# A hybrid diffusion step on one core: two output rows in the input projection, nine begun strips, two-bank scores, Hyena beside five heads, and DeltaNet's last head three steps ahead

## The chip, the cores and the metric

The kernel runs on one core of a Trainium2 chip. The core has a matrix engine (TensorE, PE in the profile; its weight loads are PEld), a vector engine (DVE), a scalar engine (ACT), a general engine (POOL, also called GpSimd) and an engine that issues DMAs (SP). Engines run beside each other; each takes its own instructions in a fixed order and waits on semaphores for the others. SBUF is the on-chip memory, PSUM the accumulator memory of eight banks that the matrix engine writes. The metric is the device time of one execution in microseconds; lower is better.

## The reference

One inference step through two layers, on 128 context tokens and 512 latent tokens (640 rows together, model width 1024), in float32. Each layer is: half a SwiGLU feed-forward block (FFN, hidden width 2816), a mixer, another half FFN, each behind an RMSNorm with shift, scale and gate from a modulation vector.

```python
# layer 0's mixer: RWKV-7 (8 heads of 64) beside gated DeltaNet (4 heads of 128), both in both directions
p = p + mu * (centred_shift(p) - p)             # RWKV's input: a token and the mean of its neighbours
qkv = silu(conv3(qkv, conv_w))                  # DeltaNet's input: a three-tap convolution
S = S*w - (S kk)(kk a) + v k                    # RWKV's state, per token
S = S * exp(gl) + k_out @ (u - w @ S)           # DeltaNet's state, per chunk of 64 tokens
# layer 1's mixer: latent attention (8 heads) beside Hyena (order 2, width 512)
s = q_nope @ k_nope.T + q_pe @ k_pe.T
prob = softmax(s * scale); o = prob @ v
z = v
for gate in (x1, x2):                           # p -> conv3 -> v, x1, x2
    z = gate * (bidir_fftconv(z, h_f, h_b) + bias * z)
```

## The kernel before

Activations stand transposed: 128 partitions of features, 640 tokens along the free axis, cut into two halves of H = 320. A float32 product is made of three products of split operands: each operand x is a high part (rounded to a matmul-ready type by ACT) and a low part (x minus the high part, by DVE or POOL). A "strip" is 128 output columns of a projection: a load of 512 KB into a tile `wr` (two of them), the split into `wh` and `wl`, then 8 x 3 matmuls per half, 48 in all, into two PSUM banks.

*Order of the work.* The program is written in Python and unrolled. A planner (line `schedule_with_timeline_sim=True`) walks it ahead of time with a model of the engines' times and fixes each engine's order; program order is the priority, and work whose inputs are not ready in that model lets later work pass. Tiles come from pools with so many buffers per tag; an instruction that needs a buffer waits for the last use of the one that it replaces.

*FFN* (`ffn`, from L640 on). Gate and up projections are multiplied by a scheme of seven half-size products per 128 hidden columns instead of eight: `quarters` (L588) forms sums and differences of the activations' quarters, on POOL, DVE and ACT, when the second half's norm is ready; `strip` (L675) forms those of the weights on POOL (L684, tile `S`) and makes seven products of 12 matmuls each. Two of the seven products need only the first half's activations. `first` (L666) makes these two ahead for the first NE = 5 strips (here "begun strips"), so that TensorE has work while `quarters` runs; the results are kept in `u2` and `s1`. A begun strip loads its gate weights again later and then has five products left, 60 matmuls. The strips come in five groups (5, 4, 4, 4, 5), each followed by its part of the down projection. Beside the FFNs of layer 0 the modulation vectors of later blocks are computed from 256 KB pieces of their weights (`wmod`); `self.bg` is the list of those still to do.

*Layer 0's mixers* (`mixers0`). The input projection makes 15 RWKV strips (`shift`) and 17 of DeltaNet (`gate`, `conv`), each via a padded copy `pp` into an output row `o` (640 tokens) that is stored to DRAM (`pd`). In `shift` POOL adds the two neighbours (`nb`, L878), ACT scales the token itself (L881) and DVE adds both with one multiply-add per piece (L882); the pieces are the context and the latent tokens. `conv` uses `conv3`: ACT scales the token (L911), and two DVE multiply-adds per piece bring the neighbours (L912, L913). The tag `o` gets its number of buffers from the first call, in `shift`, which gives none, so there is one. Between the strips the heads' preparation runs, with the inversion of triangular blocks on DVE and POOL (L824, L826).

Then the recurrences run in steps of 64 tokens, forward and backward together (`chunks`). A head pair of RWKV and a head of DeltaNet form one set and take turns within a step, eight steps over the latent tokens and two over the context; `advance` lays consecutive sets one step over each other. After a set's last step, `tail` writes the RWKV tail (L1350 on) and the DeltaNet tail (L1600 on), whose rows go to `mixd`, from where the output projection (`out_proj`) loads them, DeltaNet's last head (row 7) before RWKV's last pair (row 3).

*Layer 1's mixers* (`mixers1`). `latents` makes the attention's compressed queries and keys and the values V. Then `heads` runs eight heads; for each it projects query and key, and for five blocks of 128 queries makes scores, softmax and values. Scores of a latent block are two products of 320 keys, each in a PSUM bank of its own (tag `sc`, four banks); DVE takes the maximum of each (L1746) and joins them (L1748), ACT makes two exponentials with row sums (L1752), DVE joins the sums (L1755) and scales (L1757). TensorE transposes the probabilities, and DVE copies them out of PSUM (`PT`, L1779). Beside heads 0 to 3 stand the twelve strips of Hyena's input (`hyena_in`, tiles `pp`, `cv`), three per head; then the weight pool is closed, Hyena's constants are loaded in its place, and the long convolutions (`hyena`) stand beside heads 4 to 7, three pieces of work per head out of seven, so that they are used up in head 6.

## Time and profile before

| what | value |
| --- | --- |
| time, median of 3 runs | 3182.38 us (3175.32 to 3186.39) |
| the profiled execution | 3187.08 us, its span 3185.1 us, granted clock 0.957 |
| busy share: TensorE, DVE, ACT, POOL | 93%, 71%, 43%, 38% |
| DMA | 385.36 MB, mean 121 GB/s |

The profile is one execution. Its page gives busy time by engine, the chain of work that ended last (followed back from the last instruction, at each step to what released it) and groups of equal instructions. The trace behind it answers for any stretch of time, tile or line: a table of stretches gives for each its length, then for TensorE, its weight loads, DVE, ACT and POOL the busy time and in brackets the number of instructions, then the granted TensorE clock (1.00 is full), the share of the DMA engines' time and the rate in GB/s. In a row such as `PE ps L287 <- DVE t L1735: 5.1, 1, 5.1` the instruction named first waited for the one behind the arrow, with total, count and longest in us. In timelines the first number is the start in us from the start of the span, the second the length; brackets hold the engine's idle time before it and what ended it. All matmuls are issued on line 287.

### The profile page before, as it was taken

How to read it: one execution, taken by the hardware profiler on the slowest of the kernel's cores; microseconds unless marked ns; L12 is line 12 of the kernel's file. 1: busy time of each engine (PE TensorE's matmuls, PEld its weight loads, DVE VectorE, ACT ScalarE, POOL GpSimd, SP SyncE). 2: the span in 40 equal slices, each digit the busy share in tenths (PEclk: the TensorE clock that was granted, in tenths of full speed). 3: DMA queues.
4: the chain of work that ended last, by engine and by line, in shares of the span. 5: the costliest groups of instructions: out<-in, count | busy, mean ns of one | idle time of the engine just before them, and what ended most of it. 6: DMA issues, size and time to landing. Idle time of an engine off the chain costs nothing.

```text
span 3185.1 us, 56006 instructions
## 1 busy us (share of the span) xinstructions
PE 2958.5 (93%) x21505; PEld 2671.5 (84%) x21505; DVE 2267.1 (71%) x4011; ACT 1355.0 (43%) x2846; POOL 1200.8 (38%) x1114
## 2 busy tenths in 40 slices
PE   7799999998988998889999979999989989899998
PEld 2689999987865676879999979999979748899998
DVE  5956667668769666695666797777766786977777
ACT  3423334566365555442333453333545424433333
POOL 1733335225545220263333474444310021744442
PEclk9999999998888989889999989999999989999999
DMA  7465542455564332445553222222321215222222
GB/s 273 137 209 164 177 137 72 166 157 170 139 151 112 93 86 81 161 146 181 163 180 116 82 93 87 84 86 83 122 62 58 91 47 181 67 90 86 80 83 83
DMA packets 277587, 385.36 MB, mean 121 GB/s; under 512 B 128704, under 2 KB 161120, under 8 KB 275400
## 3 DMA queue, kind: packets, MB, share of 16 engines
q1 hardware_dynamic: 277160, 381.13, 38.3%
q8 instruction: 169, 2.77, 0.4%
q14 instruction: 98, 0.80, 0.1%
q0 software_dynamic: 160, 0.66, 0.0%
HBM read 330.29 MB, written 51.42 MB: 120 GB/s over the span
## 4 chain that ended last, share of the span: by engine, by line
PE 54%; DVE 10%; ACT 4%; DMA 4%; POOL 3%; issue 3%; SPq 1%; DVEq 0%; ACTq 0%; POOLq 0%
PE ps L287 52%; DMA wr<-in_wd_dram 2%; DVE wl L655 1%; POOL S L684 1%; DMA wr<-in_wo_dram 1%; DVE nx L539 1%; DVE wl L471 1%; POOL X L826 0%; POOL wl L655 0%; POOL inv L824 0%; PE ps L1778 0%; DMA pd<-o 0%; DVE nacc L514 0%; DVE b L605 0%; ACT wh L470 0%
## 5 line engine op out<-in xcount | busy, mean ns | idle before, releaser
L287 PE MATMUL ps<-hh,wh 128*128 128x320 f32 x2208 | 698.6, 318 | 17.8 <-DVE g L1901 7.1
L287 PE MATMUL ps<-hl,wh 128*128 128x320 f32 x2208 | 695.1, 316 | 5.4 <-POOL hl L546 2.7
L287 PE MATMUL ps<-hh,wl 128*128 128x320 f32 x2208 | 686.5, 315 | 5.3 <-DVE wl L471 4.2
L287 PE MATMUL ps<-b,wh 128*128 128x320 f32 x2112 | 480.5, 315 | 32.5 <-DVE b L605 17.2
L287 PEld LDWEIGHTS ps<-hh,wh 128*128 128x128 f32 x2208 | 422.4, 192 | 34.4 <-DVE g L1901 7.9
L287 PEld LDWEIGHTS ps<-hl,wh 128*128 128x128 f32 x2208 | 422.8, 192 | 9.7 <-POOL hl L546 3.9
L287 PEld LDWEIGHTS ps<-hh,wl 128*128 128x128 f32 x2208 | 420.3, 191 | 8.8 <-DVE wl L471 5.4
L287 PEld LDWEIGHTS ps<-b,wh 128*128 128x128 f32 x2112 | 360.7, 192 | 40.5 <-DVE b L605 19.4
L287 PE MATMUL ps<-hidl,wh 128*128 128x320 f32 x1248 | 383.7, 309 | 0.0
L287 PE MATMUL ps<-hidh,wh 128*128 128x320 f32 x1248 | 383.2, 312 | 0.0
L287 PE MATMUL ps<-hidh,wl 128*128 128x320 f32 x1248 | 381.7, 309 | 1.0 <-DVE wl L471 1.0
L550 DVE SCALAR_TENSOR_TENSOR x<-ps,mod,x 128x128 f32<-128x128 f32 (+2 forms) x528 | 212.4, 435 | 212.3 <-PE ps L287 211.7
L655 POOL TENSOR_TENSOR wl<-S,wh 128x512 fp32r<-128x512 f32 x176 | 260.5, 1480 | 264.8 <-ACT wh L654 261.6
L684 POOL TENSOR_TENSOR S<-wr,wu 128x512 f32<-128x512 f32 x88 | 125.2, 1423 | 600.9 <-DMA wr<-in_wgu_dram 394.9
L287 PE MATMUL ps<-b,wl 128*128 128x320 f32 x1056 | 330.6, 315 | 9.4 <-DVE wl L655 6.1
L470 ACT CAST wh<-wr 128x512 fp32r<-128x512 f32 (+2 forms) x210 | 157.7, 754 | 407.0 <-PE ps L287 318.0
L654 ACT CAST wh<-S 128x512 fp32r<-128x512 f32 (+1 forms) x264 | 201.0, 763 | 216.0 <-PE ps L287 163.7
L471 DVE TENSOR_TENSOR wl<-wr,wh 128x512 fp32r<-128x512 f32 (+2 forms) x210 | 186.5, 891 | 82.9 <-ACT wh L470 80.9
L287 PEld LDWEIGHTS ps<-hidh,wh 128*128 128x128 f32 x1248 | 232.9, 188 | 13.3 <-issue 7.4
L287 PEld LDWEIGHTS ps<-hidh,wl 128*128 128x128 f32 x1248 | 233.4, 188 | 1.5 <-DVE wl L471 1.5
L287 PEld LDWEIGHTS ps<-hidl,wh 128*128 128x128 f32 x1248 | 234.1, 188 | 0.0
L287 PEld LDWEIGHTS ps<-b,wl 128*128 128x128 f32 x1056 | 202.3, 192 | 13.8 <-DVE wl L655 8.5
(457 smaller groups left out, 5971.2 us busy)
## 6 DMA issues: line engine op xcount, KB each, us to landing
wmod<-in_wmod_dram SPq DMA_DIRECT2D x288, 256.0 KB
wr<-in_wgu_dram SPq DMA_DIRECT2D x108, 512.0 KB
wu<-in_wgu_dram SPq DMA_DIRECT2D x88, 512.0 KB
wr<-in_wd_dram SPq DMA_DIRECT2D x80, 320.0 KB
wr<-in_wd_dram SPq DMA_DIRECT2D x96, 256.0 KB
pd<-o SPq DMA_DIRECT2D x32, 320.0 KB
wr<-in_abg_dram SPq DMA_DIRECT2D x17, 512.0 KB
wr<-in_wo_dram SPq DMA_DIRECT2D x16, 512.0 KB
```

Of the source, the lines that this page charges most:

```text
L287: self.nc.tensor.matmul(out=out, lhsT=lhsT, rhs=rhs, start=start, stop=stop)
L470: nc.scalar.copy(out=wh, in_=w)
L471: nc.vector.tensor_sub(out=wl, in0=w, in1=wh.bitcast(F32))
L539: nc.vector.scalar_tensor_tensor(out=xn[:, a:b], in0=self.x[c][:, k, a:b], scalar=A, in1=r[:, a:b], op0=ALU.mult, op1=ALU.mult)
L550: self.nc.vector.scalar_tensor_tensor(out=self.x[c][:, d, a:b], in0=q[:, a:b], scalar=gate[:, cond, d:d + 1], in1=self.x[c][:, d, a:b], op ...
L654: nc.scalar.copy(out=hi, in_=r)
L655: eng.tensor_tensor(out=lo, in0=r, in1=f32(hi), op=ALU.subtract)
L684: G.tensor_tensor(out=out, in0=x, in1=y, op=op)
```

## The change

Five edits, none of which changes what is computed.

1. *Out rows in two places.* The row `o` of the input projection gets two buffers, taken at the pool's opening, and `shift` uses `conv3` like `conv`: the tile `nb` and POOL's sum of the neighbours go, DVE has two multiply-adds per piece in place of one.
2. *Nine begun strips.* `NE` becomes (5, 9): an FFN begins nine strips if the list of modulation work is empty when it starts, else five. Strips 5 to 8 belong to the second group.
3. *Two-bank scores.* Both halves of a block's scores stand in one tile of two banks (two such tiles); one maximum and one exponential with one row sum run over both, and the joining instructions go. From head 3 on (`NHS`) ACT copies the transposed probabilities instead of DVE.
4. *Hyena beside five heads.* One of Hyena's input strips is placed in `latents` before the values, two behind them; three heads have three strips each; the convolutions stand beside heads 3 to 7 with two pieces each. The strips' pool opens earlier, on the other side of the memory.
5. *DeltaNet's lead.* In the last set (i == 3) DeltaNet's step s stands beside RWKV's step s - 3; a `yield True`, by which `advance` counts steps, comes only when RWKV has made one.

```diff
@@ constants
-NE = 5
+NE = (5, 9)
+NHS = 3
+LEAD = 3
@@ ffn
-        early = {}
+        early, ne = {}, NE[not self.bg]
...
-            p1, s1 = tile("u2", NE), tile("s1", NE + 1)
+            p1, s1 = tile("u2", ne), tile("s1", ne + 1)
...
-                for f in range(NE):
+                for f in range(ne):
                     first(f)
@@ in_proj0
+        out_ = lambda: self.t(ip, [P, T], "o", bufs=2)
+        for _ in range(2):
+            out_()
         pp = self.pads(ip, 2)
...
-            nb = self.t(ip, [P, T + 1], "nb")
-            nc.gpsimd.tensor_tensor(out=nb, in0=p[:, 0:T + 1], in1=p[:, 2:T + 3], op=ALU.add)
-            o = self.t(ip, [P, T], "o")
-            for a, b, g in ((0, LP, 0), (LP, T, 1)):
-                nc.scalar.activation(out=o[:, a:b], in_=p[:, a + 1 + g:b + 1 + g], func=AF.Copy, scale=omu[:, mi:mi + 1])
-                nc.vector.scalar_tensor_tensor(out=o[:, a:b], in0=nb[:, a + g:b + g], scalar=hmu[:, mi:mi + 1],
-                                               in1=o[:, a:b], op0=ALU.mult, op1=ALU.add)
+            o = out_()
+            self.conv3(p, (hmu[:, mi:mi + 1], omu[:, mi:mi + 1], hmu[:, mi:mi + 1]), o)
@@ chunks
-        for s in range(NCH - PCH):
-            sets = [[(W, 1, self.gdn_step(G, PCH + s, NCH - 1 - s, W[1], s < (NCH - PCH) // 2)),
-                     (S, 1, self.rwkv_step(R, y, PCH + s, NCH - 1 - s, S[1], s < (NCH - PCH) // 2))]]
+        n, lead = NCH - PCH, LEAD if i == 3 else 0
+        half = n // 2
+        for s in range(n + lead):
+            sets, r = [[], []], s - lead
+            if s < n:
+                sets[0].append((W, 1, self.gdn_step(G, PCH + s, NCH - 1 - s, W[1], s < half)))
+            if r >= 0:
+                sets[0].append((S, 1, self.rwkv_step(R, y, PCH + r, NCH - 1 - r, S[1], r < half)))
             if s < PCH:
-                sets.append([(W, 0, self.gdn_step(G, s, PCH - 1 - s, W[0], s < PCH // 2)),
-                             (S, 0, self.rwkv_step(R, y, s, PCH - 1 - s, S[0], s < PCH // 2))])
+                sets[1].append((W, 0, self.gdn_step(G, s, PCH - 1 - s, W[0], s < PCH // 2)))
+            if 0 <= r < PCH:
+                sets[1].append((S, 0, self.rwkv_step(R, y, r, PCH - 1 - r, S[0], r < PCH // 2)))
...
-            yield True
+            if r >= 0:
+                yield True
@@ latents
         latent(0, 3, "q_norm", put_q)
+        next(strips)
...
         self.close(ap)
+        for _ in range(2):
+            next(strips)
@@ softmax
-            ss = [self.ps("sc") for _ in keys]
...
+            sc = self.psum.tile([P, 2, 512], F32, tag="sc", name=self.name("ps"), bufs=2)[:, :len(keys)]
+            n = keys[0][1]
...
+            for i, (k0, _) in enumerate(keys):
+                self.mm(sc[:, i, :n], qt[hh][:96, P * qi:P * qi + P], kt[hh][:96, k0:k0 + n])
+            nc.vector.tensor_reduce(out=mx, in_=sc[:, :, :n], axis=mybir.AxisListType.XY, op=ALU.max)
...
+            nc.scalar.activation(out=pr[:, :nk].rearrange("p (k n) -> p k n", n=n), in_=sc[:, :, :n], func=AF.Exp, scale=scale, bias=mx,
+                                 accum_out=sm)
@@ values
-                nc.vector.tensor_copy(out=PT[hh][:, g:g + n, P * (qi - 1):P * qi],
-                                      in_=q[:, :P * n].rearrange("p (k t) -> p k t", k=n))
+                (nc.vector.tensor_copy if hh < NHS else nc.scalar.copy)(out=PT[hh][:, g:g + n, P * (qi - 1):P * qi],
+                                                                        in_=q[:, :P * n].rearrange("p (k t) -> p k t", k=n))
@@ mixers1
-        self.latents(h, first)
+        sp = self.pool("strips", bufs=1, reuse_waits="tile")
+        strips = self.hyena_in(h, sp)
+        self.latents(h, first, strips)
...
-        for i in range(4):
+        for i in range(NHS):
             next(heads)
             for _ in range(3):
                 next(strips)
...
-        for i in range(4, 8):
+        for i in range(NHS, 8):
             next(heads)
-            for _ in range(3):
+            for _ in range(2):
                 next(conv, None)
```

More of the change, by code (lines that the diff above doesn't have):

```diff
@@ L690, in strip @@
             else:
-                u, g0 = tile("u2", NE), tile("s1", NE + 1)
+                u, g0 = tile("u2", ne), tile("s1", ne + 1)
                 a11, a12 = parts((g, V))
@@ L852, in gate @@
             q = self.strip(I["abg"][0], h)
-            o = self.t(ip, [P, T], "o", bufs=2)
+            o = out_()
             for c in range(2):
@@ L860, in conv @@
             q = self.strip(I["abg"][1 + i], h)
-            o = self.t(ip, [P, T], "o", bufs=2)
+            o = out_()
             if j == 3:
@@ L876, in shift @@
             self.padded(q, p)
[L877 to L883 removed]
+            o = out_()
+            self.conv3(p, (hmu[:, mi:mi + 1], omu[:, mi:mi + 1], hmu[:, mi:mi + 1]), o)
             if func is not None:
@@ L1244, in chunks @@
                         to, j, steps = run
-                        r = next(steps, False)
-                        if r is False:
+                        got = next(steps, False)
+                        if got is False:
                             runs.remove(run)
-                        elif r is not None:
-                            to[j] = r
+                        elif got is not None:
+                            to[j] = got
                     yield
+            if r == PCH - 1:
+                nc.sync.dma_start(out=self.O["s_rwkv"][:, i].rearrange("d p v -> p d v"), in_=S[0])
             if s == PCH - 1:
-                nc.sync.dma_start(out=self.O["s_rwkv"][:, i].rearrange("d p v -> p d v"), in_=S[0])
                 for d in range(2):
                     nc.sync.dma_start(out=self.O["s_gdn"][d, i], in_=W[0][d])
-            yield True
+            if r >= 0:
+                yield True
     def rwkv_step(self, X, ys, c0, c1, S, first):
@@ L1633, in small_split, with latents @@
         return out
-    def latents(self, h, first):
+    def latents(self, h, first, strips):
         nc, I = self.nc, self.I
@@ L1740, in softmax @@
             nk = sum(n for _, n in keys)
[L1741 to L1757 removed]
+            sc = self.psum.tile([P, 2, 512], F32, tag="sc", name=self.name("ps"), bufs=2)[:, :len(keys)]
+            n = keys[0][1]
+            mx = self.t(ap, [P, 1], "mxs", bufs=4)
+            sm = self.t(ap, [P, 1], "sms", bufs=4)
+            for i, (k0, _) in enumerate(keys):
+                self.mm(sc[:, i, :n], qt[hh][:96, P * qi:P * qi + P], kt[hh][:96, k0:k0 + n])
+            nc.vector.tensor_reduce(out=mx, in_=sc[:, :, :n], axis=mybir.AxisListType.XY, op=ALU.max)
+            nc.vector.tensor_scalar(out=mx, in0=mx, scalar1=-scale, scalar2=None, op0=ALU.mult)
+            pr = S[hh, qi] = self.t(ap, [P, 2 * H], "pr", bufs=2)
+            nc.scalar.activation(out=pr[:, :nk].rearrange("p (k n) -> p k n", n=n), in_=sc[:, :, :n], func=AF.Exp, scale=scale, bias=mx,
+                                 accum_out=sm)
+            nc.vector.reciprocal(out=sm, in_=sm)
+            nc.vector.tensor_scalar(out=pr[:, :nk], in0=pr[:, :nk], scalar1=sm, scalar2=None, op0=ALU.mult)
         def values(hh, qi):
@@ L1923, in hyena_in @@
                 for g, n in ((0, 4), (4, 1)):
-                    q = self.ps("tr")
+                    q = self.ps("tr" if "tr" in self.tags else "mx")
                     for j in range(n):
@@ L2116, in mixers1 @@
         self.l1 = self.pool("l1", bufs=1, reuse_waits="tile")
-        self.latents(h, first)
+        self.tc.swap_default_side()
+        sp = self.pool("strips", bufs=1, reuse_waits="tile")
+        self.tc.swap_default_side()
+        strips = self.hyena_in(h, sp)
+        self.latents(h, first, strips)
         self.banks(mm=2, sc=4, tr=2)
         ap = self.pool("heads", bufs=1, reuse_waits="tile")
-        sp = self.pool("strips", bufs=1, reuse_waits="tile")
-        heads, strips = self.heads(ap), self.hyena_in(h, sp)
-        for i in range(4):
+        heads = self.heads(ap)
+        for i in range(NHS):
             self.mark(f"head{i}")
@@ L2128, in mixers1 @@
         next(strips, None)
+        self.tc.swap_default_side()
         self.close(sp)
+        self.tc.swap_default_side()
         self.close_w()
```

15 lines of the change are left out of this document (removed).

## The prediction, made before the result was known

> **What bounds the kernel now.** I read the totals of the page first, then a table of time stretches cut at the places that the change touches (columns: length, then busy time and instruction count of the TensorE matmuls, the weight loads, DVE, ACT and POOL, then granted clock, DMA share, GB/s), then the waits, groups and timelines inside those stretches.
>
> ```profile
> PE 2958.5 (93%) x21505; PEld 2671.5 (84%) x21505; DVE 2267.1 (71%) x4011; ACT 1355.0 (43%) x2846; POOL 1200.8 (38%) x1114
> ...
> 590.00:900.00 310.00, 273.23 (x2033) 259.99 (x2033) 200.38 (x338) 168.31 (x337) 132.79 (x221) 0.92 0.52 150
> ...
> 1200.00:1252.00 52.00, 49.97 (x612) 38.32 (x612) 34.82 (x114) 32.41 (x118) 2.13 (x4) 1.00 0.24 72
> 1252.00:1300.00 48.00, 33.04 (x142) 25.36 (x142) 24.56 (x60) 18.37 (x43) 5.14 (x7) 0.65 0.47 156
> 1836.00:1890.00 54.00, 35.02 (x191) 31.64 (x190) 50.65 (x45) 30.98 (x55) 42.36 (x24) 0.81 0.30 102
> ...
> 1960.00:2006.00 46.00, 46.00 (x316) 46.00 (x315) 33.75 (x47) 19.02 (x32) 28.48 (x20) 1.00 0.24 74
> 2730.00:2760.00 30.00, 21.14 (x107) 19.47 (x106) 29.08 (x24) 16.40 (x26) 24.84 (x11) 0.83 0.19 65
> 2760.00:2800.00 40.00, 35.74 (x228) 33.11 (x227) 39.45 (x45) 13.40 (x23) 31.89 (x21) 1.00 0.28 95
> 2320.00:2372.00 52.00, 45.37 (x264) 41.48 (x263) 31.66 (x32) 20.16 (x30) 8.42 (x6) 0.97 0.24 71
> 2372.00:2517.00 145.00, 144.53 (x925) 133.37 (x926) 98.34 (x247) 72.28 (x198) 11.96 (x9) 0.99 0.15 46
> 2517.00:2658.00 141.00, 122.31 (x469) 71.18 (x468) 115.76 (x261) 33.54 (x103) 28.53 (x20) 0.94 0.26 89
> ```
>
> TensorE bounds the kernel: it is busy 93% of the span, and in the middle of an FFN (1960 to 2006) it never stops: 316 matmuls in 46 us, **0.1456 us per 128x320 matmul**. Nothing in the change lowers the number of matmuls. So each edit can win only what TensorE now loses in its stretch: 36.8 us in the input projection (310 less 273.23), 15.0 at the end of layer 0's mixers (48 less 33.04, at a clock of 0.65), 19.0 and 8.9 where the last two FFNs begin, and 6.6 + 0.5 + 18.7 = 25.8 in the attention and Hyena stage. In the two FFN beginnings DVE is full (50.65 of 54, 29.08 of 30); in the Hyena stretch it has 115.76 of 141.
>
> **Scores, strips and Hyena (2320 to 2658).** The rows are groups of DVE and ACT instructions in the Hyena stretch (count, busy, mean ns), then TensorE's waits in the three stretches.
>
> ```profile
> L1746 DVE TENSOR_REDUCE mxs<-ps 128x1 f32<-128x320 f32 (+1 forms) x35 | 15.6, 466 | 0.1
> L1779 DVE COPY PT<-ps 128x512 f32<-128x512 f32 (+1 forms) x32 | 14.4, 484 | 0.6 <-PE ps L1778 0.6
> ...
> L1755 DVE TENSOR_TENSOR sms<-sms 128x1 f32<-128x1 f32 x16 | 6.2, 388 | 1.8 <-ACT pr L1752 1.5
> ...
> L1748 DVE TENSOR_TENSOR mxs<-mxs 128x1 f32<-128x1 f32 x16 | 3.3, 206 | 0.0
> ```
> ```profile
> L1752 ACT ACTIVATE pr<-ps,mxs 128x320 f32<-128x320 f32 (+1 forms) x35 | 17.7, 510 | 46.0 <-PE ps L1778 25.3 <-DVE mxs L1749 20.7
> L1752 ACT ACTIVATION_READ_ACCUMULATOR pr<-ps,mxs 128x1 f32 x35 | 6.9, 197 | 0.0
> ...
> L1787 ACT COPY om<-ps 128x512 f32<-128x512 f32 x3 | 1.8, 586 | 22.1 <-PE ps L287 22.1
> ```
> ```profile
> PE ps L287 <- POOL acc L1660: 3.7, 1, 3.7
> ...
> PE ps L287 <- DVE t L1735: 5.1, 1, 5.1
> ...
> PE ps L287 <- DVE t L1735: 5.6, 1, 5.6
> ```
>
> Now twelve Hyena strips stand beside heads 0 to 3, where TensorE is full anyway (144.53 of 145), while heads 4 to 7 share 141 us with the whole of Hyena, where DVE lags and TensorE twice waits over 5 us for the query's rotary product queued behind Hyena's products. The change moves three strips ahead into the latents, which wait 3.7 us for a POOL sum, and gives Hyena five heads. A strip is 48 matmuls, 48 x 0.1456 = 7.0 us; a head without strips is at most (145 - 12 x 7.0) / 4 = 15.3 us of TensorE. The latents get 21 us more to do, the strip heads 36 less, the Hyena stretch 15.3 more: zero in sum, so the gain is idle time that closes.
>
> Does DVE permit it? In the Hyena stretch four heads now carry 14.4 us of copies of transposed probabilities, 6.2 and 3.3 of joining halves. From head 3 on all three leave DVE: 23.9 off. The added head brings a quarter of what stays in its groups; the reductions are 15.6 / 4 = 3.9, and I allow 10 with its other small groups. 115.8 - 23.9 + 10 = 102 us in about 141 + 15 - 15 = 141: 72%, against 82%. The merged operations are in no row. A reduction over both banks costs between one half (0.47) and two (0.93), the joint exponential between 0.51 and 2 x (0.51 + 0.20) = 1.41; I take the upper ends, so no gain for them, and the lower would free another 20 x 0.47 = 9 us of DVE. ACT takes 20 large and 20 small copies, at most 40 x 0.586 = 23 us on 33.54: it stays below half. If ACT's cover failed, those 23 us would be on the path. The moved strips issue their 512 KB loads and, for the last four, stores on SP's queue, at DMA shares of 0.24 and 0.15.
>
> TensorE keeps some idle: the last head still stands alone, and Hyena's chain still has its turns. Of 25.8 I leave 8 open: **-18**, bounds -26 (all closed) and +37 (the slower rival below).
>
> **Out rows (590 to 900).** Waits (us in total, times, longest), the two operations that change places (ns least/median/most), and pieces of the chain (start, length).
>
> ```profile
> ACT o L911 <- DMA pd<-o: 35.1, 9, 11.9
> ...
> ACT o L881 <- DMA pd<-o: 22.4, 9, 6.0
> ...
> PE ps L287 <- ACT w L1051: 10.0, 2, 9.1
> ```
> ```profile
> L913 DVE SCALAR_TENSOR_TENSOR o<-pp,cols,o x24: 247/634/911, 636.1 to 893.7; 128x128 f32<-128x128 f32 x12, 128x512 f32<-128x512 f32 x12
> ```
> ```profile
> L878 POOL TENSOR_TENSOR nb<-pp x15: 1254/1924/2235, 604.9 to 868.7; 128x641 f32<-128x641 f32 x15
> ```
> ```profile
> 739.80 5.13 DMA pd<-o
> ...
> 836.02 4.53 DMA pd<-o
> ...
> 895.96 2.42 DMA pd<-o
> ```
>
> One row `o` holds a finished strip until its store has landed; ACT, in order, waits over 57 us for it, and behind ACT once TensorE (9.1 us). On the chain these stores stand for 5.13 + 4.53 + 2.42 = 12.1 us. With a second row, a store has a whole strip more, 7.0 us, to land in 5.1. That removes at most 12.1. The sum of neighbours leaves POOL (15 x 1.924 = 28.9 us, POOL also solving the block inverses there) and becomes one more multiply-add per piece on DVE: 30 x 0.634 = 19.0 us. DVE has 200 of 310 us, so it lies beside TensorE; uncovered it would be +19.0 - 12.1 = +7. I take **-7**, bounds -12 and +7. The weight loads issue on SP behind the same stores as before; nothing new queues there.
>
> **The last head's lead (1200 to 1300).** DVE instructions (start, length): the RWKV state's last write, DeltaNet's state writes, the ends of both tails.
>
> ```profile
> 1250.33 0.46 DVE L1326 SCALAR_TENSOR_TENSOR S<-ps,eG,Se 128x64 f32<-128x64 f32 x2
> ...
> 1263.26 0.35 DVE L1584 SCALAR_TENSOR_TENSOR W<-W,eGl,ps 128x128 f32<-128x128 f32 x1 [0.75 <-PE ps L287]
> ...
> 1267.92 0.49 DVE L1371 TENSOR_TENSOR ys<-ys,ps 128x320 f32<-128x320 f32 x1 [1.27 <-PE ps L287]
> ...
> 1271.10 0.35 DVE L1584 SCALAR_TENSOR_TENSOR W<-W,eGl,ps 128x128 f32<-128x128 f32 x1 [0.25 <-PE ps L287]
> ...
> 1278.33 0.48 DVE L1623 SCALAR_TENSOR_TENSOR tt<-ps,cols,tt 128x64 f32<-128x64 f32 x2 [0.63 <-PE ps L1618]
> ```
>
> The last row is the end of DeltaNet's tail, at 1278.8; RWKV's tail ended at 1268.4, 17.6 us after its state at 1250.8. DeltaNet's state came 20.6 us later. Three steps of lead turn this round: DeltaNet's tail runs under RWKV's last steps, and RWKV's tail ends the stage. If RWKV isn't delayed, the stage ends 10.4 us earlier; if both end in the middle, RWKV 10.3 later, nothing is gained. If DeltaNet's three steps simply go first at their latency, 3 x 7.8 (1263.26 to 1271.10), RWKV ends at 1250.8 + 23.5 and the stage at 1291.9: +13. TensorE was full at 1200 to 1252, so some delay is sure: **-4**, bounds -10 and +13. The states' stores move with their own recurrence on SP's queue; they are late for nobody.
>
> **Nine begun strips (1836 and 2730).**
>
> ```profile
> L655 DVE TENSOR_TENSOR wl<-S,wh x88: 1206/1210/2290, 123.9 to 3122.8; 128x1024 fp32r<-128x1024 f32 x88
> ```
> ```profile
> 2742.62 0.48 DVE L673 TENSOR_TENSOR s<-ps,u 128x320 f32<-128x320 f32 x1
> 2743.02 1.48 DVE L605 TENSOR_TENSOR b<-hidh,b 128x1280 fp32r<-128x1280 f32 x1
> ...
> 2749.76 4.87 DVE L605 TENSOR_TENSOR b<-hidh,b 128x1280 fp32r<-128x1280 f32 x2 [0.92 <-ACT b L604]
> ```
> ```profile
> L415 SPq DMA_DIRECT2D wmod<-in_wmod_dram x288: 327/382/1672, 7.1 to 1715.7; - x144
> ```
>
> The two subtractions of one shape show why DVE is full here: alone the 128x1280 form takes 1.48 us, beside POOL 4.87 / 2 = 2.43. The Trainium skill, page "SBUF — State Buffer", section "Who interferes with whom", says that a DVE instruction with two SBUF inputs and a GpSimd one that reads SBUF exclude each other; by that rule the trace agrees, and it speaks against bringing more such splits into this place. It would give the upper of the prices that follow; the row's own spread gives them without it.
>
> The modulation weights are all loaded by 1715.7, so the list is empty at 1836 and 2730 and both of layer 1's FFNs begin nine strips; layer 0's keep five. Four more bring 96 matmuls (14.0 us) forward, plus four loads of 512 KB that are read twice. On DVE each brings a split of weights (1.21 to 2.29) and an addition (0.48) forward: 6.8 to 11.1 us, on an engine that has 3.4 us free in the first beginning and 0.9 in the second. So the beginning ends 3 to 10 us later. Later the four strips have 60 matmuls instead of 84; a begun strip takes 40 x 60 / 228 = 10.5 us (DVE-bound), a whole one 46 x 84 / 316 = 12.2, so 6.8 us come back, not 14. That is 6.8 - 3.4 - 6.8 = -3.4 and -0.9 with the low price: **-4** together; bounds -28 (2 x 14.0, if both engines had room) and +8 (2 x 11.1 - 2 x 6.8). Queued behind the four loads on SP is strip 0's, which POOL needs first.
>
> **Sum.** -18 - 7 - 4 - 4 = -33 on the profiled execution's 3187.08 us (span 3185.1 and 2.0 around it): 3154.1. The runs' median, 3182.38, lies 4.7 below the profiled execution; so 3149.4 for the median, 3149.
>
> **Rivals.**
> 1. *The idle moves on* (16 in 100). In the Hyena stretch a head's own chain takes over: ACT's copies and the joint exponential in one queue, TensorE waiting for probabilities. For it: ACT there waits 25.3 us for transposes and 20.7 for maxima. Against: no TensorE wait on exponentials in the listed waits. The -18 falls to -3, with DVE's extra work in the input projection eating half its -7: 3182.4 - 3 - 3.5 - 4 - 4 = 3168 at best, and with the begun strips at +8 3180: no change or barely faster.
> 2. *The scores' banks* (9 in 100, slower). Two one-bank tiles per block now fall free one by one; the pair falls free only after one joint exponential, and the maximum starts only after the second product. If TensorE has nothing else queued before the next scores, each of 32 wide blocks costs 0.51 + 0.20 + 0.47 = 1.18 us: +37.7. It decides from the point where TensorE waits for ACT in front of scores. Against: 925 matmuls at 144.53 of 145 with the present chain. 3149.4 + 18 + 37.7 = 3205.
> 3. *The begun strips lock with POOL* (5 in 100 as the deciding part). Each of DVE's added splits takes its longest length while POOL reads beside it: +8 by the bound, and if strip 0's loads come four turns later another 4 x 2.29 in each FFN, +26 in all instead of -4: 3149.4 + 30 = 3179, no change. The Trainium skill ("SBUF — State Buffer", "Who interferes with whom") has this exclusion as a rule.
> 4. *The lead does not lead*: order is planned ahead, and the steps could be put back where they were. 0 instead of -4, 3153; inside the forecast.
>
> **Chances.** Forecast with its own range 3120 to 3170: 70 in 100; rival 1: 16, rival 2: 9, rival 3: 5. About 0.3%, 9.5 us, is what a measurement can tell from no change. Faster (below 3172.8): 0.70 and half of rival 1, 0.78; slower (above 3191.9): 0.08; the same: 0.14. The range goes from 3120 (a further 29: idle all closed in the attention stage -8, stores -5, lead -6, strips -10) to 3182, the upper end of rival 1.
>
> **What would show it.** Right: no ACT waits on `pd<-o` above 2 us each; TensorE idle under 10 us from the latents to the end of attention; DeltaNet's tail done before RWKV's; matmuls in the two FFN beginnings where TensorE stood. Wrong: TensorE waiting for exponentials, begun strips spaced over 11 us in the second group, DVE in front of TensorE in the input projection, or RWKV's last state after 1270.

## The result and the profile after

The changed kernel takes 3154.74 us (median of 4 runs, 3151.82 to 3158.72) against 3183.58 for the kernel before beside it (3175.32 to 3186.39): a ratio of **0.9914**, 95% interval 0.9892 to 0.9936. The ratio makes it some 27 us less, the two medians 28.8. The profiled execution took 3158.72 us, its span 3157.0 at a granted clock of 0.962. The forecast of 3149 lies 6 us below; the sum was nearly right. Its terms were not: two of the four were worth nothing that can be measured, and one of the two priced lowest brought about half of the gain. That the sum came out is luck.

Totals of the page after. DVE did 35.5 us less than before and POOL 25; TensorE has the same 21505 matmuls and is busy 13.6 us less, at a mean clock of 0.962 against 0.957.

```profile
PE 2944.9 (93%) x21505; PEld 2662.6 (84%) x21505; DVE 2231.6 (71%) x3905; ACT 1363.8 (43%) x2823; POOL 1175.8 (37%) x1099
```

To see where the time went I cut both executions at DVE instructions that stand in both: the last reciprocal of the norm ahead of layer 0's mixers, the last written out row, the last tail, the norm ahead of layer 1's first FFN, the norm ahead of the latents, the first split for the output projection, and the final norm (start, length, instruction). The first fence is the timeline of the kernel before; its out row (893.7) and last tail (1278.33) are quoted in the prediction. The second is the changed kernel.

```profile
591.09 2.15 DVE L514 RECIPROCAL nacc<-nacc 128x320 f32<-128x320 f32 x1 [4.15 <-ACT nacc L513]
...
1851.32 2.15 DVE L514 RECIPROCAL nacc<-nacc 128x320 f32<-128x320 f32 x1 [0.29 <-ACT nacc L513]
...
2286.97 2.15 DVE L514 RECIPROCAL nacc<-nacc 128x320 f32<-128x320 f32 x1 [0.89 <-ACT nacc L513]
...
2662.18 1.69 DVE L476 TENSOR_TENSOR hl<-m,hh 128x320 fp32r<-128x320 f32 x4
...
3162.28 2.15 DVE L514 RECIPROCAL nacc<-nacc 128x320 f32<-128x320 f32 x1 [0.89 <-ACT nacc L513]
```
```profile
592.50 2.15 DVE L516 RECIPROCAL nacc<-nacc 128x320 f32<-128x320 f32 x1 [4.15 <-ACT nacc L515]
...
879.40 0.75 DVE L914 SCALAR_TENSOR_TENSOR o<-pp,cols,o 128x512 f32<-128x512 f32 x1
...
1272.76 0.48 DVE L1633 SCALAR_TENSOR_TENSOR tt<-ps,cols,tt 128x64 f32<-128x64 f32 x2 [0.63 <-PE ps L1628]
...
1849.26 2.15 DVE L516 RECIPROCAL nacc<-nacc 128x320 f32<-128x320 f32 x1 [0.29 <-ACT nacc L515]
...
2279.24 2.15 DVE L516 RECIPROCAL nacc<-nacc 128x320 f32<-128x320 f32 x1 [0.88 <-ACT nacc L515]
...
2641.51 1.69 DVE L478 TENSOR_TENSOR hl<-m,hh 128x320 fp32r<-128x320 f32 x4
...
3134.14 2.15 DVE L516 RECIPROCAL nacc<-nacc 128x320 f32<-128x320 f32 x1 [0.89 <-ACT nacc L515]
```

The differences of these rows are the stages in the table. The other rows are the same cuts through the profiles of the experiments that follow; the last column is each run's ratio to the kernel before, timed beside it, with its interval. "Rows" is the part of the front up to the last out row.

| kernel | rows | front, to the last tail | first FFN of layer 1 | attention and Hyena | output projection and second FFN, to the final norm | ratio |
| --- | --- | --- | --- | --- | --- | --- |
| before | 302.6 | 687.7 | 435.6 | 375.2 | 500.1 | 1 |
| changed | 286.9 | 680.7 | 430.0 | 362.3 | 492.6 | 0.9914 (0.9892 to 0.9936) |
| five begun strips (ne5) | 285.6 | 680.2 | 433.6 | 365.8 | 500.4 | 0.9968 (0.9956 to 0.9980) |
| nine places, five begun (buf9) | 286.2 | 675.4 | 434.3 | 366.9 | 500.5 | 0.9956 (0.9939 to 0.9972) |
| eleven begun, no lead (ne11_no_lead) | 286.3 | 677.4 | 427.2 | 362.2 | 488.0 | 0.9880 (0.9861 to 0.9899) |
| no lead | 288.6 | 680.7 | 431.0 | 364.3 | 491.6 | 0.9912 (0.9896 to 0.9927) |
| old rows | 303.2 | 677.9 | 429.8 | 367.3 | 491.6 | 0.9941 (0.9923 to 0.9958) |
| one place | 303.3 | 692.2 | 432.1 | 361.0 | 491.9 | 0.9936 (0.9919 to 0.9953) |
| old rows, no lead (old_front) | 302.8 | 673.4 | 430.4 | 365.0 | 492.8 | 0.9919 (0.9903 to 0.9936) |
| old attention and Hyena (old_mla) | 285.9 | 674.5 | 430.1 | 378.0 | 493.3 | 0.9963 (0.9950 to 0.9975) |
| old scores | 286.5 | 675.5 | 427.4 | 375.8 | 491.5 | 0.9943 (0.9927 to 0.9959) |
| copies on DVE (pt_dve) | 286.4 | 679.0 | 428.8 | 371.9 | 491.1 | 0.9929 (0.9912 to 0.9945) |
| Hyena beside four heads (hyena4) | 286.7 | 671.8 | 428.9 | 363.3 | 492.2 | 0.9922 (0.9908 to 0.9936) |
| no maxima (no_max) | 286.4 | 683.2 | 428.4 | 359.7 | 491.6 | 0.9901 (0.9884 to 0.9919) |

The table is the main instrument of this study: a stage that keeps its instructions shows how far it moves by itself. The second FFN with nine begun strips takes 491.1 to 493.3 us in ten profiles, with five 500.1 to 500.5 in three: 8.3 us, far outside the scatter; the first FFN takes 427.4 to 432.1 with nine, 433.6 to 435.6 with five. ("Second FFN" in what follows includes the output projection ahead of it.) The front, with instructions in the same order in eight profiles (changed, ne5, buf9, old_mla, old_scores, pt_dve, hyena4, no_max), takes 671.8 to 683.2: there a difference of 7 us between two profiles proves nothing.

The front's column stops at the last tail, and that flatters the new rows. In the changed kernel the first weights of the output projection that follows land only after the tails, as ACT's wait for them shows; with the old rows (before, old_rows, old_front) the same instruction stands 3.2 us ahead of the last tail's end and waits for nothing.

```profile
1273.91 1.04 ACT L472 CAST kh<-wr 128x1024 fp32r<-128x1024 f32 x1 [1.26 <-DMA wr<-in_wo_dram]
```

From the norm to the first split for that projection it is 687.6 us before, 683.8 changed, and 673.3 with the whole front as before (old_front).

The two stretches in which TensorE stood before, as tables of stretches: first the FFN beginning of layer 1's first FFN, before and after; then the attention stage after, begun and divided at the same events as in the prediction's table, and the input projection (length, busy time and count of TensorE, its weight loads, DVE, ACT, POOL, then clock, DMA share, GB/s).

```profile
1850.00:1870.00 20.00, 18.97 (x115) 18.25 (x114) 17.78 (x20) 12.04 (x21) 10.96 (x5) 0.91 0.32 105
1870.00:1890.00 20.00, 10.67 (x51) 9.21 (x50) 18.97 (x10) 9.67 (x12) 19.92 (x9) 0.74 0.15 52
```
```profile
1850.00:1870.00 20.00, 17.45 (x110) 16.66 (x109) 19.33 (x20) 15.07 (x24) 5.63 (x2) 0.96 0.23 79
1870.00:1890.00 20.00, 16.89 (x99) 16.12 (x100) 12.70 (x14) 9.88 (x17) 8.34 (x5) 0.91 0.50 158
...
2312.20:2385.00 72.80, 70.16 (x446) 66.74 (x445) 42.53 (x52) 33.50 (x59) 8.74 (x6) 1.00 0.24 75
2385.00:2490.00 105.00, 104.86 (x674) 95.62 (x673) 65.64 (x147) 47.85 (x117) 8.72 (x7) 1.00 0.14 44
2490.00:2642.00 152.00, 132.11 (x542) 80.71 (x540) 110.57 (x211) 54.00 (x135) 32.90 (x22) 0.97 0.27 92
...
590.00:900.00 310.00, 273.63 (x2064) 258.31 (x2063) 215.55 (x376) 174.40 (x356) 121.40 (x230) 0.93 0.53 155
```

The latents are now full (70.16 of 72.8, where 45.37 of 52 stood), and the FFN beginning holds 209 matmuls in 40 us in place of 166. In the Hyena stretch TensorE still stands 19.9 of 152 us; DVE has 110.57 there, 73%, close to the predicted 72%, and yet TensorE waits. The prediction's table stops 4.2 us ahead of the first split for the output projection; with the same end for both, half a microsecond behind that split, the whole stage before and after is:

```profile
2320.00:2662.70 342.70, 313.11 (x1658) 246.53 (x1657) 248.56 (x544) 129.06 (x334) 48.91 (x35) 0.96 0.22 70
2312.20:2642.00 329.80, 307.13 (x1658) 243.07 (x1656) 218.74 (x408) 135.35 (x310) 50.37 (x35) 0.99 0.22 73
```

The same 1658 matmuls: of 12.9 us, 6.9 were idle time of TensorE (29.6 to 22.7) and 6.0 busy time, at a clock of 0.99 in place of 0.96.

### The profile page after: what moved, and what is told of

It reads as the page before. It is cut to its first block, busy times and chain, and to the rows that moved or that the text cites. A ratio compares the mean times of both kernels' runs of the same rounds, so it can differ in the third digit from the quotient of the medians.

```text
span 3157.0 us, 55877 instructions
## 1 busy us (share of the span) xinstructions
PE 2944.9 (93%) x21505; PEld 2662.6 (84%) x21505; DVE 2231.6 (71%) x3905; ACT 1363.8 (43%) x2823; POOL 1175.8 (37%) x1099
## 4 chain that ended last, share of the span: by engine, by line
PE 47%; DVE 9%; DMA 3%; issue 2%; ACT 2%; POOL 1%; SPq 0%; DVEq 0%; ACTq 0%; POOLq 0%
PE ps L289 46%; DMA wr<-in_wd_dram 2%; DVE wl L657 1%; DMA wr<-in_wo_dram 1%; DVE nx L541 1%; DVE wl L473 0%; DVE hidl L478 0%; DVE nacc L516 0%; PE ps L1788 0%; DVE nacc L508 0%; DVE u L689 0%; DVE nx L712 0%; ACT wh L656 0%; DVE b L607 0%; DVE nsq L689 0%
## 5 line engine op out<-in xcount | busy, mean ns | idle before, releaser
L289 PE MATMUL ps<-hh,wh 128*128 128x320 f32 x2208 | 693.4, 316 | 14.3 <-DVE g L1912 7.1
L289 PEld LDWEIGHTS ps<-hh,wl 128*128 128x128 f32 x2208 | 418.4, 191 | 13.1 <-DVE wl L657 6.0
L289 PEld LDWEIGHTS ps<-hl,wh 128*128 128x128 f32 x2208 | 420.6, 191 | 10.1 <-DVE hl L607 3.9
```

The lines of the kernel that those rows point to most:

```text
L289: self.nc.tensor.matmul(out=out, lhsT=lhsT, rhs=rhs, start=start, stop=stop)
```

## The experiments

**1. Begun strips.** Three kernels: five begun strips again; nine places for their parts but five begun; eleven begun (without the lead of the last head, for which experiment 2 shows no gain; it has eleven places as well).

```diff
-NE = (5, 9)
+NE = (5, 5)      # ne5
+NE = (5, 11)     # ne11_no_lead, with LEAD = 0
@@ buf9
-                for f in range(ne):
+                for f in range(5):
```

> The changed kernel with five begun strips in both FFNs of layer 1 again; all else stays changed. Theory (the two traces): nine begun strips won 4.9 us in the first of these FFNs and 8.3 in the second, so without them the time is 3154.7 + 13 = 3168, ratio to the kernel before about 0.9955. Rival (the price of the prediction, DVE-bound): they won 4 in all: 3159, ratio 0.993.

> The changed kernel with nine places for the parts of begun strips in layer 1, but only five strips begun. Theory (work carried ahead): the gain is the 96 matmuls brought forward, the places alone bring nothing, so the ratio to the kernel before is that of the run with five begun strips, 0.997. Rival (the places): strips that are further apart no longer wait for a place to come free, and the ratio is that of the changed kernel, 0.9914.

> The changed kernel with eleven begun strips in layer 1's FFNs and without the lead of the last head. Theory (work carried ahead pays as long as TensorE stands still in the beginning): four strips won 13 to 17 us in two FFNs, 1.6 to 2.1 each per FFN; about 8.5 and 7 us of idle are left there beside the wait for the first product, so two more strips win half to all of that rate, 3 to 8 us: ratio 0.9912 less 0.001 to 0.0025, about 0.9895. Rival (DVE, full in the beginning, is the bound and two more splits of 1.2 us each are simply added): the ratio stays at 0.9912 or rises to 0.992.

With five the ratio is 0.9968, and both FFNs fall back to their old length. The theory holds and the prediction's price does not: by the stages nine strips are worth 434.5 - 429.7 = 4.8 us (means of three and ten profiles) and 8.3 us. Places alone bring nothing: 434.3, 500.5 and 0.9956, as with five. Eleven bring a further 2.5 and 4.0 us and the fastest kernel of the study, 0.9880, median 3143.07 against 3178.63 beside it. Per strip that is (2.5 + 4.0) / 2 = 3.3 us over both FFNs, against 13.1 / 4 = 3.3 from five to nine: no sign of a price that rises. But eleven is one profile, and its 427.2 in the first FFN lies only 0.2 below the shortest with nine; the second FFN, 3.1 below, and the ratio carry the reading.

Where it comes back is read from the ends of the strips. The timelines give the first of the two multiplications that close a strip (L708), for strips 4, 5, 8 and 9 of the second FFN: first with five begun strips, then with nine.

```profile
2788.72 0.48 DVE L708 TENSOR_TENSOR nsq<-nsq,s 128x320 f32<-128x320 f32 x1
2833.60 1.57 DVE L708 TENSOR_TENSOR nsq<-nsq,s 128x320 f32<-128x320 f32 x1
...
2869.34 0.48 DVE L708 TENSOR_TENSOR nsq<-nsq,s 128x320 f32<-128x320 f32 x1
2911.03 1.58 DVE L708 TENSOR_TENSOR nsq<-nsq,s 128x320 f32<-128x320 f32 x1
```
```profile
2791.07 0.48 DVE L708 TENSOR_TENSOR nsq<-nsq,s 128x320 f32<-128x320 f32 x1
2831.91 1.07 DVE L708 TENSOR_TENSOR nsq<-nsq,s 128x320 f32<-128x320 f32 x1
...
2862.82 0.48 DVE L708 TENSOR_TENSOR nsq<-nsq,s 128x320 f32<-128x320 f32 x1
2901.33 1.58 DVE L708 TENSOR_TENSOR nsq<-nsq,s 128x320 f32<-128x320 f32 x1
```

Counted from the output projection's first split (2643.14 and 2641.51), strip 4 gets there at 145.6 with five and 149.6 with nine: the beginning is **4.0 us later**. Then across the down projection to strip 5: 44.9 against 40.8, 4.0 back. Strips 5 to 8: 35.7 against 30.9, 4.8 back. To strip 9, across the next down projection: 41.7 against 38.5, 3.2 back. In sum 12.0 of the 14.0 us of matmuls that were carried forward come back. In the first FFN the same four steps are 9.4 later, and 3.8, 6.1 and 3.1 back. That TensorE had room in the beginning shows in its counts up to strip 4: 921 matmuls in 149.6 us, 142.8 busy at a clock of 0.96, in place of 831 in 145.6, 130.7 busy at 0.92.

One reason why the beginning got only 4 to 9 us later is seen in the splits themselves: the row of the nine weight splits in the first FFN's beginning (least, median, most in ns), then timeline rows of DVE and of POOL there.

```profile
L657 DVE TENSOR_TENSOR wl<-wr,wh x9: 1209/1214/3820, 1834.7 to 1878.8; 128x1024 fp32r<-128x1024 f32 x9
```
```profile
1866.42 3.82 DVE L657 TENSOR_TENSOR wl<-wr,wh 128x1024 fp32r<-128x1024 f32 x1
```
```profile
1866.24 2.91 POOL L620 TENSOR_TENSOR hidl<-hidl,hidh 128x1280 f32<-128x1280 f32 x1 [13.52 <-DVE hidh L618]
```

More than half of the splits took 1.21 us, eight of the nine at most 1.9. The one of 3.82 started 0.2 us into a POOL sum of 2.91. (The second FFN has one like it: 3.55 us, begun 1.4 us into a sum of 3.83.) POOL was busy only 5.63 and 8.34 us in the two stretches of 20: it stood waiting for DVE's quarters (13.52 us) while the begun strips were split. The Trainium skill ("SBUF — State Buffer", "Who interferes with whom") has the exclusion of a DVE instruction with two SBUF inputs and a GpSimd one that reads SBUF as a rule; the trace agrees in these two rows, and shows that there was little POOL work to exclude.

**2. The lead.**

```diff
-LEAD = 3
+LEAD = 0
```

> The changed kernel with DeltaNet's and RWKV's steps of the last head side by side again. Theory: on the two chains the loads of the output weights set the start of the output projection, and the stage moved by 1 us only beyond what it had inherited: 3154.7 + 1 = 3156, ratio 0.992. Rival (the prediction): the lead is worth 4: 3159, ratio 0.993. If the weights' loads are what waits, the last tails end later by some 5 us in this run's trace and the output projection still starts within 2 us of where it does in the changed kernel.

0.9912: no difference. Timeline rows of the last state writes and tails, first of the changed kernel, then without the lead:

```profile
1250.82 0.48 DVE L1336 SCALAR_TENSOR_TENSOR S<-ps,eG,Se 128x64 f32<-128x64 f32 x2
...
1260.22 0.35 DVE L1594 SCALAR_TENSOR_TENSOR W<-W,eGl,ps 128x128 f32<-128x128 f32 x1
...
1269.56 0.49 DVE L1381 TENSOR_TENSOR ys<-ys,ps 128x320 f32<-128x320 f32 x1
```
```profile
1264.28 0.35 DVE L1594 SCALAR_TENSOR_TENSOR W<-W,eGl,ps 128x128 f32<-128x128 f32 x1 [0.76 <-PE ps L289]
...
1272.40 0.48 DVE L1633 SCALAR_TENSOR_TENSOR tt<-ps,cols,tt 128x64 f32<-128x64 f32 x2 [0.63 <-PE ps L1628]
```

The lead does move DeltaNet's last state, by 4 us against this run (1264.28 to 1260.22), and RWKV isn't delayed. Most of the change is not the lead's, though: without it DeltaNet's last state already comes 13.3 us after RWKV's, where it was 20.6 before, and beside the old rows (old_rows) the lead leaves it at 20.9. But DeltaNet's tail, free to run at 1260.6, ends at 1273.2, behind RWKV's at 1270.1, just as without the lead (1272.9). In the changed kernel DeltaNet's pieces stand behind RWKV's in the engines' order: TensorE's transposes for it (L1628) start at 1270.10, right after DVE's last subtraction for RWKV (L1381, 1269.56). I had expected the tails to end 5 us later without the lead; they don't. The first split for the output projection stands at 1276.3 and 1277.0, within the 2 us expected if the weights' loads are what waits; and by the row of ACT's wait, weights that land at 1273.9 leave an earlier tail little to win.

**3. The out rows.** Old rows; one place with the sum on DVE; and old rows without the lead, the whole front as before.

```diff
@@ old_rows; old_front has LEAD = 0 as well
-            o = out_()
-            self.conv3(p, (hmu[:, mi:mi + 1], omu[:, mi:mi + 1], hmu[:, mi:mi + 1]), o)
+            nb = self.t(ip, [P, T + 1], "nb")
+            nc.gpsimd.tensor_tensor(out=nb, in0=p[:, 0:T + 1], in1=p[:, 2:T + 3], op=ALU.add)
+            o = self.t(ip, [P, T], "o")
...
@@ one_place
-            o = out_()
+            o = self.t(ip, [P, T], "o")
```

> The changed kernel with the RWKV input projection as before: one place for the out row, the sum of neighbours on POOL. Theory: the input projection ended 10.2 us earlier on the chain, of which 4.2 were left after the preparation of head 2, and 4 to 6 stay to the end: 3154.7 + 5 = 3160, ratio 0.993. Rival 1 (the bound of the prediction): all of the stores' 12 us stay: 3167, ratio 0.995. Rival 2: nothing stays, since the preparation of the heads is bound by its own chain: 3155, ratio 0.9914.

> The changed kernel with RWKV's rows in one place again, while the sum of neighbours stays a second multiply-add on DVE. With one place and the sum on POOL the last row was written 302.6 and 303.2 us after the norm, in the changed kernels 285.7 to 288.7. Theory (the place is what was waited for, 12.1 us of stores on the chain; DVE's form alone wins the other 4): 296 to 300 us. Rival (POOL's sum was late, not the place): 286 to 290. At the end of the program 10 of the 16 us are lost in the preparation of the heads in both cases: ratio 0.991 to 0.994.

> The changed kernel with the old input rows and without the lead: layer 0's mixers entirely as before, the rest changed. From the norm ahead of the input projection to the last head's tails, the kernel before took 687.7 us, the eight runs with new rows took 674.5 to 683.2, old rows with the lead 677.9. Theory (the front is worth something, but either part alone catches most of it): 684 to 691 us here, ratio 0.9945 to 0.9955. Rival (687.7 was chance: the same code spreads over 9 us): 675 to 683 us here, and the ratio is that of the old rows with the lead or below, 0.992 to 0.994.

The second place is needed for the earlier rows: with one place and the sum on DVE the last row comes at 303.3, as late as with POOL's sum (302.6 to 303.2), and not at the 296 to 300 that I had expected. With two places it comes at 285.6 to 288.6. (Two places with POOL's sum were not tried, so whether the place alone is enough stays open.) In the waits of the changed kernel's input projection ACT now waits for stores five times, 17.6 us in all, where the two rows quoted in the prediction had 18 times and 57.5 us:

```profile
ACT o L912 <- DMA pd<-o: 10.5, 3, 7.8
...
ACT o L870 <- DMA pd<-o: 7.1, 2, 3.9
```

But 16 us earlier rows make no earlier end. The front as before takes 673.4 us, among the shortest of all, and the kernel 0.9919. So the theory that either part alone catches most of a gain falls, and the rival holds: the 687.7 of the kernel before were chance. (The intervals of 0.9919 and 0.9914 leave room for some microseconds either way.) Old rows with the lead (0.9941) and one place (0.9936) read 0.002 slower than that; the intervals overlap, and whether the lead hurts beside a single place stays open. Where the 16 us go can be followed. Most are lost in the heads' preparation. The rows are the last instruction of the third of four block inversions on POOL, first with the old front, then changed:

```profile
1021.75 0.21 POOL L826 TENSOR_TENSOR inv<-iv,X 120x8 f32<-120x8 f32 x1
```
```profile
1017.71 0.21 POOL L826 TENSOR_TENSOR inv<-iv,X 120x8 f32<-120x8 f32 x1
```

Counted from the norm (591.60 and 592.50) it stands at 430.2 and 425.2: of 16 us, 5 are left, and at the same place in the fourth inversion 3.7 (547.3 and 543.6). That this inversion paces the heads' preparation is read from the traces, not tried.

The rest, and nearly all that the 687.7 stand above the 673.4, goes in the recurrences, and there the stretch is long where TensorE's clock is low. These rows of the table of stretches run from the 36th to the 54th of the 72 writes of RWKV's state: before, old front, changed.

```profile
1106.10:1191.00 84.90, 77.18 (x961) 58.55 (x960) 55.78 (x179) 41.90 (x143) 25.29 (x60) 0.82 0.31 83
1106.20:1178.00 71.80, 65.78 (x963) 50.02 (x962) 55.53 (x180) 41.86 (x144) 25.20 (x61) 1.00 0.37 98
1099.00:1184.00 85.00, 77.95 (x946) 58.61 (x946) 58.52 (x190) 40.99 (x138) 28.01 (x69) 0.82 0.30 80
```

The first two kernels have the same instructions in the same order on DVE, ACT and POOL through the whole front, and 13.1 of the 14.3 us between them lie in this stretch, at a clock of 0.82 in one execution and 1.00 in the other. The changed kernel had 0.82 and so lost more here than it had kept. With the old rows two profiles of three have 1.00 here; all eleven with the sum on DVE have 0.78 to 0.87. Whether the new rows bring the lower clock about, and with it eat their own gain, was not tried.

**4. Attention and Hyena.** All of it as before; then single parts undone: the scores, the copies, the fifth head. And one kernel with the maxima left out.

```diff
@@ pt_dve
-                (nc.vector.tensor_copy if hh < NHS else nc.scalar.copy)(out=PT[hh]...
+                nc.vector.tensor_copy(out=PT[hh]...
@@ hyena4
-        for i in range(NHS):
+        for i in range(4):
...
-            for _ in range(3):
+            for _ in range(3 if i < 3 else 0):
...
-        for i in range(NHS, 8):
+        for i in range(4, 8):
...
-            for _ in range(2):
+            for _ in range(3):
@@ no_max
-            nc.vector.tensor_reduce(out=mx, in_=sc[:, :, :n], axis=mybir.AxisListType.XY, op=ALU.max)
-            nc.vector.tensor_scalar(out=mx, in0=mx, scalar1=-scale, scalar2=None, op0=ALU.mult)
+            mx = zero                          # and scale = 1e-3 * 96.0 ** -0.5
@@ old_scores: softmax as in the kernel before; old_mla: latents, heads, strips and Hyena too
```

> The changed kernel with attention and Hyena as before: one-bank scores, copies of transposed probabilities on DVE, all twelve strips beside heads 0 to 3, Hyena beside heads 4 to 7. Theory (the two traces): this part won 12.9 us between the norm before the latents and the output projection: 3154.7 + 13 = 3168, ratio 0.9955. Rival (the prediction): 18, so 3173, ratio 0.997.

> The changed kernel with the copies of the transposed probabilities on DVE in all heads. In the Hyena stretch that puts 40 copies, about 18 us, back on DVE and takes 15.8 off ACT. Theory (DVE holds TensorE up there although it is busy only 73% of the stretch, because Hyena's products come in bunches): 6 to 10 us slower than the changed kernel, ratio 0.9935 to 0.9945. Rival (DVE has room): no difference, 0.9914.

> Leaves out the maxima of the scores: the 40 reductions and their scalings on DVE are gone, the exponentials take a bias of zero and a scale a thousandth of the right one. That takes 24 x (0.73 + 0.15) = 21 us from DVE in the Hyena stretch and the wait of ACT for them. Theory (DVE's bunches): TensorE's idle there falls from 19.9 us to 8 or 10 and the time by 10: ratio 0.988. Rival (Hyena's chain of turns and the loads at the end hold TensorE up, not DVE): idle falls by less than 4 us, ratio 0.990 or more.

> The changed kernel with the scores in two one-bank tiles, the maxima and exponentials in halves as before; copies on ACT, early strips and Hyena beside five heads stay. From the norm ahead of the latents to the output projection's operands, runs with this part changed take 362.2 to 367.3 us (mean 364.8), the old part 375.2 and 378.0, copies on DVE 371.9. Theory (the copies are 7 of 12, the merged operations the rest of DVE's relief: 0.73 against 2 x 0.47 + 0.21 us per block): 367 to 370 us, ratio 0.9925 to 0.993. Rival 1 (the pair of banks released as one costs as much as the merging wins): 363 to 366, 0.9914. Rival 2 (the second slower case of the prediction at work): faster than 362, 0.990.

> The changed kernel with Hyena beside heads 4 to 7 again, three steps for each; strips in the latents, copies and scores stay changed. Theory (the copies and the filled latents are the gain; a fifth head beside Hyena brings little, since TensorE still loses 19.9 us there): 364 to 368 us for the stage, ratio 0.991 to 0.9925. Rival (the fifth head gives TensorE work while DVE lags): 370 to 374 us, ratio 0.9935 or more.

The stage takes 361.0 to 367.3 us in the eight profiles that keep all of this part, mean 364.4; as before it takes 375.2 and 378.0, mean 376.6. So the part is worth **12.2 us**, as the theory of the two traces said, not 18. Undone singly, the parts don't add up: the scores cost 375.8 - 364.4 = 11.4 us, the copies 7.5, the fifth head nothing (363.3). These are single profiles against a scatter of 6.3 us; by the ratios of the whole kernel the scores cost 9 us and the copies 5, the latter with overlapping intervals. The strips in the latents were not undone alone. Undoing either of the first two gives back most of the gain. For the scores none of my three expectations was right: the joined operations, which I had taken as neutral, carry it, together with the two-bank tiles that they need. Their rows, first before, then changed (ns, least/median/most):

```profile
L1746 DVE TENSOR_REDUCE mxs<-ps x72: 276/483/503, 2380.6 to 2641.1; 128x1 f32<-128x320 f32 x64, 128x1 f32<-128x128 f32 x8
...
L1752 ACT ACTIVATE pr<-ps,mxs x72: 367/527/543, 2382.8 to 2646.0; 128x320 f32<-128x320 f32 x64, 128x128 f32<-128x128 f32 x8
```
```profile
L1761 DVE TENSOR_REDUCE mxs<-ps x40: 277/818/825, 2387.8 to 2621.6; 128x1 f32<-128x640 f32 x32, 128x1 f32<-128x128 f32 x8
...
L1764 ACT ACTIVATE pr<-ps,mxs x40: 367/794/811, 2390.7 to 2626.3; 128x640 f32<-128x640 f32 x32, 128x128 f32<-128x128 f32 x8
```

Per block: 0.82 us in place of 2 x 0.48, and 0.79 in place of 2 x 0.53.

How it reaches TensorE is in the Hyena stretch, from its first transform to the first split of the output projection. One row each of the table of stretches: changed, old scores, copies on DVE, no maxima.

```profile
2499.00:2641.50 142.50, 123.11 (x493) 73.34 (x491) 102.79 (x193) 47.93 (x120) 32.68 (x22) 0.97 0.25 84
```
```profile
2485.80:2642.50 156.70, 134.42 (x497) 77.82 (x495) 112.00 (x251) 52.48 (x156) 31.02 (x22) 0.91 0.23 79
```
```profile
2494.80:2647.60 152.80, 129.65 (x497) 76.23 (x495) 114.91 (x235) 33.77 (x81) 32.71 (x22) 0.94 0.24 80
```
```profile
2498.40:2639.40 141.00, 126.24 (x497) 74.56 (x495) 89.52 (x152) 47.37 (x121) 31.73 (x21) 0.96 0.25 84
```

With as good as the same matmuls, old scores lengthen this stretch by 14.2 us: idle time grows by only 2.9 (19.4 to 22.3), TensorE's *busy* time by 11.3, at a clock of 0.91 in place of 0.97. The waits are only part of the price; after them the matmuls run slower. The groups of the score products show it, changed and old scores: as many, of the same shape, at 434 and 495 ns in the mean.

```profile
L289 PE MATMUL ps<-k,q 96*128 96x320 f32 x64 | 19.8, 434 | 1.4 <-ACT pr L1764 1.4
```
```profile
L289 PE MATMUL ps<-k,q 96*128 96x320 f32 x64 | 24.5, 495 | 1.3 <-ACT pr L1766 1.3
```

The mean clocks by themselves would make 123.1 us into 123.1 x 0.97 / 0.91 = 131.2, an estimate of 8 of the 11.3. With old scores, slices of 10 us:

```profile
2580.00:2590.00 10.00, 10.00 (x34) 5.47 (x33) 10.00 (x23) 3.74 (x13) 1.90 (x2) 1.00 0.35 106
2590.00:2600.00 10.00, 5.33 (x26) 3.88 (x24) 9.87 (x22) 2.71 (x8) 3.75 (x3) 0.87 0.00 0
2600.00:2610.00 10.00, 8.65 (x32) 6.95 (x32) 9.79 (x21) 3.04 (x10) 6.24 (x5) 0.62 0.01 2
```

DVE is full over 30 us, TensorE stands, and then has a clock of 0.62. The Trainium skill ("TensorE: Matmul & The Clock Gate", "What's actually happening") states a half rate after an idle window of about 3.4 us; the trace agrees in kind: TensorE's longest gap in these slices is 3.1 us, and the clock falls during it. So DVE does hold TensorE up in bunches while its mean is 72%. But DVE's load alone isn't the answer: no maxima takes 13.3 us off it here and wins 4.7 us of the stage (359.7), half of what I expected and, with overlapping intervals of the ratios (0.9901 and 0.9914), not clear of noise; TensorE's idle falls to 14.8, not to 8 or 10. Whether the block's shorter chain or DVE's smaller load does more was not separated.

## Why the prediction was right in sum and wrong in its terms

**Out rows, -7: the step was right locally, its gain was off the path.** The 12.1 us of stores on the chain were real; the rows even came 16 us earlier, above my bound of 12. The step that failed is the one that carried this to the end unexamined: of the 16 us, 5 were left behind the third block inversion and 3.7 behind the fourth, the recurrences lost more than that at a clock of 0.82, and nothing measurable stayed (old front 0.9919, changed 0.9914). TensorE's idle time in the input projection, out of which the 7 us were to come, hardly changed either: 36.8 of 310 us before, 36.4 after. The sign "no ACT waits on `pd<-o` above 2 us each" failed as well: 7.8 and 3.9 are left.

**The lead, -4: 0.** RWKV was not delayed, as hoped, and DeltaNet's state came earlier. What failed is "DeltaNet's tail runs under RWKV's last steps": it ended 3 us behind RWKV's tail. The 10.4 us between the tails, on which the gain was built, was no accident of one profile: the old front has 10.1 and the old rows with the lead 10.4. With the sum on DVE it is 3.2 in every profile, with the lead or without, so it closed by another edit, and beside the old rows rival 4 came true: the lead did not lead. And behind the tails the output projection waited for its weights, which the sum left out.

**Begun strips, -4: -13.** The mis-sized term is "6.8 us come back". I took the strip interval of a DVE-bound first group, 10.5 us, for strips 5 to 8 as well. Inside their group the intervals are indeed 12.7, 11.2 and 7.0, which I had named as proof against the edit. But two of the three savings lie outside those intervals, across the two down projections, in which TensorE sets the pace and not DVE: in the second FFN TensorE is busy all of the 40.8 and 38.5 us, DVE 21.3 and 23.1, while between strips 5 and 8 DVE has 29.2 of 30.9. 12.0 and 13.0 us came back. The delay of the beginning, 3 to 10 us predicted, was 4.0 and 9.4. More matmuls where TensorE stood: right (51 to 99 in one stretch). Rival 3, the lock with POOL, did not come about.

**Scores, strips, Hyena, -18: -12.2.** The latents closed as predicted, and rival 2, the banks, was refuted by its own undoing: one-bank scores are slower. Two steps failed. "I take the upper ends, so no gain": the joined operations are worth as much as the whole part. And "Of 25.8 I leave 8 open": TensorE's idle in the three stretches is still 2.6 + 0.1 + 19.9 = 22.7, so "TensorE idle under 10 us" is wrong; part of rival 1 happened. The gain came by another way: I counted TensorE's idle time as all that can be won, though the rows showed a clock of 0.94, and of the 12.9 us between these two profiles 6.0 are busy time at a better clock. Hyena beside a fifth head, the visible half of the edit, brings nothing that shows.

**Sum.** -12.2 - 13.1 and nothing from the front is -25; the runs say some -27. That 3149 came close is luck, due to errors of opposite signs: the begun strips brought 9 us more than predicted, the front 11 less and attention 6 less.

## What to carry to other kernels

Price carried-ahead work over the whole way to where its absence is felt, beyond the stage in which it would have stood: it comes back where the bound engine is full. Before you credit a stage with a local gain, name the chain that comes after it, and take a second profile of the stage to see its scatter, and the clock in both. Where TensorE stands and stutters, add to its idle time the busy time that it spends below full clock.

## What the runs showed of the hardware that was not expected

With the same instructions in the same order, the front with its many small transfers and turns between engines took 671.8 to 683.2 us in eight profiles, 1.7%, while an FFN of 492 us stayed within 2.2 and one of 430 within 4.7. The clock is much of it: in two kernels with the same front, 961 and 963 matmuls took 84.9 us at a clock of 0.82 and 71.8 at 1.00.

One operation over two PSUM banks is cheaper than two: a DVE maximum 0.82 against 2 x 0.48 us, an ACT exponential 0.79 against 2 x 0.53, each without the second row sum and the joining instruction.

The same 493 to 497 matmuls took 123.1 to 134.4 us of busy time, at clocks of 0.97 to 0.91: a reading of TensorE as busy hides up to 11 us in a stretch of 157, some 8 of them by the mean clocks.
